# A hybrid attention layer on one core: another form and place for the layer norm's last steps, and another written order of the steps before it

## The chip, the cores and the metric

The kernel runs on one core of one Trainium2 chip. Its engines are named as the profile names them: PE multiplies matrices, and PEld is its loading of weights; DVE (VectorE) and ACT (ScalarE) work element by element; POOL (GpSimd) does so too and issues some of the transfers; SP issues the others. SBUF is the memory that all of them use, PSUM the memory into which PE writes. The metric is the device time of one execution in microseconds (us); lower is better.

## The reference

One layer for 512 tokens of width 1024: a projection, three mixers (an attention of three branches for 6 heads, a stick-breaking attention for 4, a gated recurrence for 6), gates, an output projection with the residual, and a layer norm.

```python
def layer_norm(v, g, b):
    v32 = v.astype(jnp.float32)
    mu = jnp.mean(v32, axis=-1, keepdims=True)
    var = jnp.mean(jnp.square(v32 - mu), axis=-1, keepdims=True)
    return ((v32 - mu) * lax.rsqrt(var + LN_EPS) * g + b).astype(v.dtype)

def reference(x, w_in, cmp_pos, w_ck1, w_ck2, w_cv1, w_cv2, hg_lb, hg_norm_w,
              w_out, ln_g, ln_b, rel_bias):
...
        h = x @ w_in[l]
...
        o_nsa = nsa_mixer(nsa_q, nsa_kc, nsa_vc, nsa_ks, nsa_vs, nsa_kw, nsa_vw, nsa_g,
                          cmp_pos[l], w_ck1[l], w_ck2[l], w_cv1[l], w_cv2[l], rel_bias)
        o_sb = stick_breaking_mixer(sb_q, sb_k, sb_v)
        o_hg = hgrn2_mixer(hg_q, hg_f, hg_i, lb_all[l])
...
        mixed = jnp.concatenate([o_nsa * jax.nn.silu(nsa_z),
                                 o_sb * jax.nn.silu(sb_z),
                                 o_hg.astype(x.dtype) * jax.nn.silu(hg_z)], axis=-1)
        x = layer_norm(ALPHA * x + (mixed @ w_out[l]).astype(x.dtype), ln_g[l], ln_b[l])
    return x
```

## The kernel before, in words

Every large product is computed in three products of rounded parts: a matrix is split into a high part `hi` (ACT rounds it) and a low part `lo` (what is left), and hi·hi, hi·lo and lo·hi are summed in PSUM. `SPLITS` says for each group of weights, first half and second half, who makes `lo`: 0 is POOL, 1 is DVE, and 3 (also the default) is ACT, which writes -hi, and a transfer issued by POOL that adds the raw weights to it.

The work is cut into steps, written as Python generators: `x`, `hf1`, `hq`, `hi`, `sq` and the like are blocks of the projection, `p0` to `p2` the pairs of heads of the recurrence, `s0` to `s3` and `v0` to `v3` the stick-breaking heads, `ck`, `cv`, `c0`, `c1`, `n0` to `n11` and `w0` to `w11` the attention, `o0` and `o1` the parts of the output projection that need only the last five of eight row blocks, and `end` the rest of it with the layer norm. The string `ORDER` lists in which order the steps advance; a name with L ahead starts a load. A scheduler then makes each engine's own order from it: what is written earlier has priority, and what stands under `high_priority` goes ahead of it where it is ready. At run time each engine takes its instructions strictly in that order and waits where one isn't ready.

`ENGINES` says for small operations whether DVE ('v'), POOL ('p') or ACT ('a') does them: `hq` and `hv0` to `hv2` copy blocks of the projection out of PSUM, `kb0` to `kb2` are the sums `nk` of the recurrence, `qs1` a product in it, `mz2` a gate product ahead of `end`.

`end` multiplies four tiles of 128 tokens (`i` is 0 to 3) by two halves of the width (`half`), adds each to `y[i, half]` in SBUF, and takes the layer norm of a tile when both halves are there. `norm_stats` sums on DVE (`bn`, then `mv`) and gets `rs`, the reciprocal root, from ACT. `norm_apply` scales and shifts y on ACT, multiplies by `ln_g` and adds `ln_b`, on DVE or POOL, and sends y out; for the last tile DVE does it all, in four instructions of two steps each. The gains `ln_g` and shifts `ln_b` lie in SBUF as four tiles named `ln`. The last half of the last tile comes from PE in two parts of 256 columns.

Of the kernel before, what the change touches and what calls it, by code (L numbers as in the profile page):

```python
# [14 lines left out]
ALU = mybir.AluOpType  # L15
# [8 lines left out]
NT = S // P  # L24
# [28 lines left out]
)  # L53

ORDER = (
# [7 lines left out]
)  # L63

BUFS = dict(at=3, g2=33, kkp=4, ma=2, mb=4, nb=2, p0=1, p5=4, psa=3, psc=1, raw=3, sa=8, sb=6, ta=8, tb=10, ti=1,
    w=16)

SPLITS = dict(ck=(0, 1), cv=(0, 1), hf1=(1, 1), hi=(3, 0), hi_sv=(0, 3), hq=(0, 0), hz=(1, 3), kw_sz=(1, 1),
    o0=(1, 3), o2=(0, 0), o3=(1, 1), sk=(3, 1), sq=(1, 3), sv_vs=(3, 1), vc_ks=(1, 3))

FROM_DRAM = ('sq', 'sk', 'q', 'q_kc', 'o0', 'o2', 'o4', 'o6')

ENGINES = dict(cl='p', e20='v', e21='p', hq='a', hs='v', hv0='v', hv1='a', hv2='a', k1='a', kb0='v', kb1='v',
    kb2='v', kd0='v', kt='v', mz0='v', mz1='v', mz2='p', mz3='v', mz4='v', nw0='v', nw1='v', nw2='v', q1='p', qs0='p',
    qs1='p', qs2='p', tmpta='a', tmptb='v', ts='p', z0='v', z1='a', z2='a', z3='v')
POOL_TILES = (1, 3)
LN_VECTOR = ((0, 1), (2, 0), (2, 1))
WARM = 8
LEVELS = (64, 32, 16, 8, 4, 2, 1)
PLAIN = 32  # L80
# [46 lines left out]
class Net:  # L127
# [777 lines left out]
    def norm_stats(self, i):  # L905
        nc = self.nc
        n = S // 2 if i == NT - 1 else S
        st = self.small((P, DM // n, 6), s="bn")
        for e in range(DM // n):
            c = e * n % S  # L910
            nc.vector.bn_stats(out=st[:, e, :], in_=self.y[i, e * n // S][:, c:c + n])
        mv = self.small((P, 2), s="mv")
        nc.vector.bn_aggr(out=mv, in_=st)
        rs = self.small((P, 1), s="rs")
        nc.scalar.activation(rs, mv[:, 1:2], AF.Ln, bias=self.eps_ln)
        nc.scalar.activation(rs, rs, AF.Exp, scale=-0.5)
        nm = self.small((P, 1), s="nm")
        if i == NT - 1:
            nc.vector.tensor_scalar(out=nm, in0=mv[:, 0:1], scalar1=-1.0, scalar2=None, op0=ALU.mult)
        else:  # L920
            nc.vector.tensor_scalar(out=nm, in0=mv[:, 0:1], scalar1=rs, scalar2=-1.0, op0=ALU.mult, op1=ALU.mult)
        return rs, nm

    def norm_apply(self, i, rs, nm):
        nc = self.nc
        y = [self.y[i, e] for e in range(2)]
        for e in range(2):
            if i == NT - 1:
                nc.vector.scalar_tensor_tensor(out=y[e], in0=y[e], scalar=nm, in1=self.lng[e], op0=ALU.add, op1=ALU.mult)
                nc.vector.scalar_tensor_tensor(out=y[e], in0=y[e], scalar=rs, in1=self.lnb[e], op0=ALU.mult, op1=ALU.add)  # L930
            else:
                nc.scalar.activation(y[e], y[e], AF.Identity, scale=rs, bias=nm)
                eng = nc.vector if (i, e) in LN_VECTOR else nc.gpsimd
                eng.tensor_tensor(out=y[e], in0=y[e], in1=self.lng[e], op=ALU.mult)
                nc.gpsimd.tensor_tensor(out=y[e], in0=y[e], in1=self.lnb[e], op=ALU.add)
            nc.sync.dma_start(out=self.out[0, i * P:(i + 1) * P, e * S:(e + 1) * S], in_=y[e])


# [230 lines left out]
    def do_end(self):  # L1169
        nc, a = self.nc, self.a  # L1170
        self.lng, self.lnb = [], []
        for l, n in ((self.lng, "ln_g"), (self.lnb, "ln_b")):
            for e in range(2):
                t = self.g2(s="ln")
                nc.sync.dma_start(out=t, in_=a[n][0:1, e * S:(e + 1) * S].broadcast_to([P, S]))
                l.append(t)
        ws = [self.out_weights(0, 2, half) for half in range(2)]
        mid = [self.out_weights(2, 1, half) for half in range(2)]
        for kt in range(3):
            self.do_m(kt)  # L1180
        st = {}
        for i in range(NT):
            for half in range(2):
                self.out_part(i, half, {0: ws[half]}, {2: mid[half]}, 2 if (i, half) == (NT - 1, 1) else 1)
            st[i] = self.norm_stats(i)
            if i:
                self.norm_apply(i - 1, *st[i - 1])
        self.norm_apply(NT - 1, *st[NT - 1])


def build(tc, a, out):
# [31 lines left out]
```

## Time and profile before

| what | value |
|---|---|
| time, median of 3 runs | 369.04 us (368.83 to 369.29) |
| the profiled execution's own time | 368.77 us |
| its span, first to last instruction | 366.9 us |
| outside the span | 1.9 us |
| PE busy | 343.1 us (94%) |
| DVE busy | 276.8 us (75%) |
| ACT busy | 248.1 us (68%) |
| POOL busy | 103.8 us (28%) |
| TensorE clock granted, mean | 0.99 |

The span is the time on the core; the runs' time adds some 2 us around it. Busy shares are means over stages with different limits, and PE's busy time counts products that overlap, so it is no measure of PE at its best rate.

### The profile page before, as it was taken

Reading aid. Unit: us, or ns where it says so; the run is one execution under the profiler, and the core shown is the slowest. Engines: PE = TensorE matmul, PEld = TensorE weight load, DVE = VectorE, ACT = ScalarE, POOL = GpSimd, SP = SyncE. Lnnn points to the kernel's source line nnn. Section 1 sums busy time; section 2 is a strip of 40 time slices with the busy share of each in tenths; the row PEclk is TensorE's granted clock in tenths of the full one; section 3 lists DMA queues with packets and bytes.
Section 4 is the critical chain, followed back from the end, with each engine's and each line's share of the span. In section 5 each row is a group of like instructions: output and inputs, shape, how many; then the busy total and the mean of one; then the engine's idle time right before and its main releaser. Section 6 shows DMA issues by size and latency. Waiting matters only on the chain.

```text
span 366.9 us, 5871 instructions
## 1 busy us (share of the span) xinstructions
PE 343.1 (94%) x2002; PEld 290.4 (79%) x2002; DVE 276.8 (75%) x628; ACT 248.1 (68%) x559; POOL 103.8 (28%) x145
## 2 busy tenths in 40 slices
PE   7999999999999998998999998999999899999980
PEld 5787899887888876876788997977877777888870
DVE  2769666689699888898876666788999657732796
ACT  3696963728559998785396777688889988731240
POOL 4065560001201111020471332242131604031092
PEclk9999999999999999999999999999999999999995
DMA  7767365250415472051348619500040698961023
GB/s 244 264 230 198 103 187 155 80 138 2 114 59 126 106 181 49 0 134 41 103 137 210 184 33 223 174 29 2 29 107 10 128 250 223 289 179 22 1 88 143
DMA packets 16910, 45.64 MB, mean 124 GB/s; under 512 B 2786, under 2 KB 3298, under 8 KB 16880
## 3 DMA queue, kind: packets, MB, share of 16 engines
q1 hardware_dynamic: 13568, 33.65, 27.5%
q0 software_dynamic: 3312, 11.61, 17.8%
q8 instruction: 16, 0.26, 0.3%
q14 instruction: 14, 0.11, 0.1%
HBM read 37.27 MB, written 2.14 MB: 107 GB/s over the span
## 4 chain that ended last, share of the span: by engine, by line
PE 56%; DVE 14%; ACT 11%; issue 10%; DMA 5%; POOL 3%; SPq 0%; DVEq 0%; POOLq 0%; ACTq 0%
PE pi L329 16%; PE pi L345 11%; PE pi L902 10%; PE pc L402 3%; PE ma L811 3%; DMA lo<-raw 3%; PE ma L377 2%; PE mb L395 2%; PE pi L316 2%; DVE sr L702 2%; DVE qz L806 2%; DMA xt<-xt 2%; ACT hi L273 2%; DVE att L820 1%; ACT pt L650 1%
## 5 line engine op out<-in xcount | busy, mean ns | idle before, releaser
L329 PE MATMUL pi<-xh,hi 128*128 128x512 f32 x160 | 47.8, 406 | 1.8 <-DVE vs L186 1.3
L329 PE MATMUL pi<-xh,lo 128*128 128x512 f32 x160 | 46.5, 396 | 1.4 <-DMA lo<-raw 1.4
L329 PE MATMUL pi<-xl,hi 128*128 128x512 f32 x160 | 46.6, 397 | 0.0
L902 PE MATMUL pi<-hi,mx 128*128 128x512 f32 (+1 forms) x134 | 40.9, 383 | 0.0
L329 PEld LDWEIGHTS pi<-xh,lo 128*128 128x128 f32 x160 | 29.3, 188 | 7.4 <-DMA lo<-raw 2.2
L329 PEld LDWEIGHTS pi<-xh,hi 128*128 128x128 f32 x160 | 28.5, 189 | 7.4 <-DVE vs L186 1.7
L329 PEld LDWEIGHTS pi<-xl,hi 128*128 128x128 f32 x160 | 29.3, 188 | 5.4
L186 DVE TENSOR_TENSOR pl<-mb,ph 128x384 fp32r<-128x384 f32 (+1 forms) x48 | 28.1, 595 | 6.8 <-ACT ph L185 6.3
L345 PE MATMUL pi<-lo,xh 128*128 128x256 f32 (+1 forms) x160 | 27.6, 286 | 1.5 <-DMA lo<-raw 1.3
L345 PE MATMUL pi<-hi,xh 128*128 128x256 f32 (+1 forms) x160 | 28.1, 290 | 0.6 <-DVE vs L186 0.6
L902 PEld LDWEIGHTS pi<-hi,mx 128*128 128x128 f32 x134 | 24.8, 188 | 4.5
L273 ACT CAST hi<-raw 128x1024 fp32r<-128x1024 f32 (+2 forms) x23 | 23.3, 1013 | 7.0 <-PE pi L902 2.8
L680 POOL TENSOR_SCALAR pt<-pt,sm,gates 128x256 f32<-128x256 f32 (+1 forms) x24 | 17.6, 740 | 33.5 <-DVE sm L677 29.3
L345 PE MATMUL pi<-hi,xl 128*128 128x256 f32 (+1 forms) x160 | 26.7, 284 | 0.0
L650 ACT ACTIVATE pt<-pt,mn 128x256 f32<-128x256 f32 (+3 forms) x42 | 24.5, 586 | 2.4 <-DVE mn L648 2.2
L902 PE MATMUL pi<-lo,mx 128*128 128x512 f32 (+1 forms) x67 | 25.8, 385 | 0.0
L185 ACT CAST ph<-mb 128x384 fp32r<-128x384 f32 (+1 forms) x48 | 24.0, 508 | 1.5 <-PE mb L395 1.3
L345 PEld LDWEIGHTS pi<-hi,xh 128*128 128x128 f32 x160 | 23.0, 190 | 1.6 <-DVE vs L186 0.8
L345 PEld LDWEIGHTS pi<-lo,xh 128*128 128x128 f32 x160 | 22.7, 191 | 1.9 <-DMA lo<-raw 1.5
L811 PEld LDWEIGHTS ma<-qz,kz 128*128 128x128 f32 x168 | 20.8, 191 | 3.7 <-ACT kz L795 1.1
L648 DVE CUSTOM_DVE_ANT_0 pt<-ma,nb 128x256 f32<-128x256 f32 (+3 forms) x42 | 21.2, 511 | 3.4 <-PE ma L377 3.3
L811 PE MATMUL ma<-qz,kz 128*128 128x128 f32 x168 | 22.7, 279 | 1.0 <-ACT kz L795 0.4
(269 smaller groups left out, 845.9 us busy)
## 6 DMA issues: line engine op xcount, KB each, us to landing
raw<-w_in SPq DMA_DIRECT2D x28, 512.0 KB, 3.6
lo<-raw POOLq DMA_DIRECT2D x9, 512.0 KB, 5.1
lo<-w_in POOLq DMA_DIRECT2D x6, 512.0 KB, 5.4
raw<-w_out SPq DMA_DIRECT2D x6, 512.0 KB, 5.1
lo<-w_out POOLq DMA_DIRECT2D x5, 512.0 KB, 5.4
y<-x SPq DMA_DIRECT2D x8, 256.0 KB, 4.2
out<-y SPq DMA_DIRECT2D x8, 256.0 KB, 2.0
xt<-xt SPq DMA_DIRECT2D x3, 512.0 KB, 7.2
```

Of the source, the lines that this page charges most:

```text
L185: nc.scalar.copy(hi, src)
L186: nc.vector.tensor_tensor(out=lo, in0=src, in1=hi.bitcast(F32), op=ALU.subtract)
L273: nc.scalar.copy(hi, raw)
L316: self.nc.tensor.matmul(ps, w[:, c0:c0 + P], self.xpart(x, kt), start=(n == 0 and j == 0), stop=(n == len(parts) - 1 and j == len(js) - 1))
L329: self.nc.tensor.matmul(ps, w[:, b * P:(b + 1) * P], self.xpart(x, kt), start=(n == 0 and j == 0), stop=(n == len(grp) - 1 and j == len(js ...
L345: self.nc.tensor.matmul(ps[:, :w_], self.xpart(x, kt)[:, i * P:(i + 1) * P], w[:, :w_], start=(j == 0), stop=(j == len(js) - 1))
L402: nc.tensor.matmul(acc[:, j * P:], vt[j], t[:, b:b + w], start=(first and j == 0 and t is h), stop=(last and j == 3 and t is l))
L648: nc.vector.tensor_tensor_reduce(out=dst, in0=src, in1=self.nb[h][:, n - 1::-1], scale=1.0, scalar=3e38, op0=ALU.add, op1=ALU.min, accum_o ...
L650: nc.scalar.activation(dst, dst, AF.Exp, bias=mn, scale=-1.0, accum_out=sm)
L680: (nc.gpsimd if i in POOL_TILES else nc.vector).tensor_scalar(out=pts[i], in0=pts[i], scalar1=sm[:, i:i + 1], scalar2=self.gates[:, i, c:c ...
L811: nc.tensor.matmul(ps[:, c * P:(c + 1) * P], kk[:, c * P:(c + 1) * P], qz[:, c, :, :].rearrange("p h t -> p (h t)"), start=True, stop=True)
L902: nc.tensor.matmul(ps, m, w[:, cs], start=(j == 0), stop=(j == len(jobs) - 1))
```

## The change

It does four things. The gains and shifts of the layer norm are also copied to PSUM (four new ACT instructions, tiles of the pool `mb`), and DVE's instructions of the layer norm read them there, while POOL's read the tiles in SBUF as before; which engine multiplies and adds for each tile and half stays as it was (`LN_FORM` writes out what `LN_VECTOR` and the test for the last tile said). In `end`, the statistics and the four last instructions of tile 3 are written under high priority. The tables `SPLITS` and `ENGINES` change: DVE takes over the `hq` copies and the `hv1` copies from ACT, and `qs1` and `mz2` from POOL; POOL takes `kb0` and `kb2` from DVE; the low parts of `hi`, `hi_sv`, `sq`, `o2` and of the second half of `o6` get other makers. And `ORDER` is another string. In all, DVE gets 11 instructions more (641 for 630), ACT 4 fewer, POOL 4 fewer, PE the same 1860 in the program.

```diff
 ORDER = (
-    "x Lhf1 Lhq 4*hf1 3*hq Lhi_sv 3*hi_sv Lhi hi_sv p1 hi Lsq hq hi p1 p0 hi 2*p1 const p1 hi 3*p1 sq p1 p0 sq 2*p0 "
+    "x Lhf1 Lhq 4*hf1 3*hq 3*hi_sv Lhi hi_sv Lhi_sv p1 hi hq hi Lsq 2*p1 p0 hi 2*p1 const p1 hi 3*p1 p0 2*sq Lsk sq "
...
-    "n10 n11 2*w9 n11 w9 m3 n10 n11 nz n10 w10 n11 2*w10 w11 nz w11 nz Lnz w11 o0 nz 3*o0 4*o1 end "
+    "2*n10 2*w9 2*n11 n10 m3 n11 nz w9 w10 n11 2*w10 w11 Lnz 2*nz w11 nz o0 w11 2*o0 o1 o0 3*o1 end "
...
-SPLITS = dict(ck=(0, 1), cv=(0, 1), hf1=(1, 1), hi=(3, 0), hi_sv=(0, 3), hq=(0, 0), hz=(1, 3), kw_sz=(1, 1),
-    o0=(1, 3), o2=(0, 0), o3=(1, 1), sk=(3, 1), sq=(1, 3), sv_vs=(3, 1), vc_ks=(1, 3))
+SPLITS = dict(ck=(0, 1), cv=(0, 1), hf1=(1, 1), hi=(0, 3), hi_sv=(1, 3), hq=(0, 0), hz=(1, 3), kw_sz=(1, 1),
+    o0=(1, 3), o2=(1, 1), o3=(1, 1), o4=(3, 3), o6=(3, 1), sk=(3, 1), sq=(3, 1), sv_vs=(3, 1), vc_ks=(1, 3))
...
-ENGINES = dict(cl='p', e20='v', e21='p', hq='a', hs='v', hv0='v', hv1='a', hv2='a', k1='a', kb0='v', kb1='v',
-    kb2='v', kd0='v', kt='v', mz0='v', mz1='v', mz2='p', mz3='v', mz4='v', nw0='v', nw1='v', nw2='v', q1='p', qs0='p',
-    qs1='p', qs2='p', tmpta='a', tmptb='v', ts='p', z0='v', z1='a', z2='a', z3='v')
+ENGINES = dict(cl='p', e20='v', e21='p', hq='v', hs='v', hv0='v', hv1='v', hv2='a', k1='a', kb0='p', kb1='v',
+    kb2='p', kd0='v', kh='a', kt='v', mz0='v', mz1='v', mz2='v', mz3='v', mz4='v', nw0='v', nw1='v', nw2='v', q1='p',
+    qs0='p', qs1='v', qs2='p', tmpta='a', tmptb='v', ts='p', z0='v', z1='a', z2='a', z3='v')
...
-LN_VECTOR = ((0, 1), (2, 0), (2, 1))
+LN_FORM = (("pp", "vp"), ("pp", "pp"), ("vp", "vp"), ("s", "s"))
...
-            if i == NT - 1:
-                nc.vector.scalar_tensor_tensor(out=y[e], in0=y[e], scalar=nm, in1=self.lng[e], op0=ALU.add, op1=ALU.mult)
-                nc.vector.scalar_tensor_tensor(out=y[e], in0=y[e], scalar=rs, in1=self.lnb[e], op0=ALU.mult, op1=ALU.add)
+            m = LN_FORM[i][e]
+            if m == "s":
+                nc.vector.scalar_tensor_tensor(out=y[e], in0=y[e], scalar=nm, in1=self.lngp[e], op0=ALU.add, op1=ALU.mult)
+                nc.vector.scalar_tensor_tensor(out=y[e], in0=y[e], scalar=rs, in1=self.lnbp[e], op0=ALU.mult, op1=ALU.add)
             else:
                 nc.scalar.activation(y[e], y[e], AF.Identity, scale=rs, bias=nm)
-                eng = nc.vector if (i, e) in LN_VECTOR else nc.gpsimd
-                eng.tensor_tensor(out=y[e], in0=y[e], in1=self.lng[e], op=ALU.mult)
-                nc.gpsimd.tensor_tensor(out=y[e], in0=y[e], in1=self.lnb[e], op=ALU.add)
+                for f, g, gp, op in zip(m, (self.lng[e], self.lnb[e]), (self.lngp[e], self.lnbp[e]), (ALU.mult, ALU.add)):
+                    if f == "v":
+                        nc.vector.tensor_tensor(out=y[e], in0=y[e], in1=gp, op=op)
+                    else:
+                        nc.gpsimd.tensor_tensor(out=y[e], in0=y[e], in1=g, op=op)
...
+        self.lngp, self.lnbp = [], []
+        for l, lp in ((self.lng, self.lngp), (self.lnb, self.lnbp)):
+            for t in l:
+                lp.append(self.ps("mb"))
+                nc.scalar.copy(lp[-1], t)
...
-            st[i] = self.norm_stats(i)
-            if i:
+            if i == NT - 1:
+                with self.tc.high_priority():
+                    st[i] = self.norm_stats(i)
                 self.norm_apply(i - 1, *st[i - 1])
-        self.norm_apply(NT - 1, *st[NT - 1])
+                with self.tc.high_priority():
+                    self.norm_apply(i, *st[i])
+            else:
+                st[i] = self.norm_stats(i)
+                if i:
+                    self.norm_apply(i - 1, *st[i - 1])
```

Three places show what this makes of the engines' orders. The first is DVE at the very end. Tile 3 is `y_3777` and `y_3873` before, `y_3815` and `y_3872` after; the two halves of tile 2 are `y_3758` with `y_3854` or `y_3853`; `pi` is PE's result, `ln` and `mb` are the gains and shifts. Before:

```order
L903 SCALAR_TENSOR_TENSOR y_3873<-y_3873,pi_4060 128x256
L911 BN_STATS bn_4082<-y_3777 128x6
L911 BN_STATS bn_4082<-y_3873 128x6
L903 SCALAR_TENSOR_TENSOR y_3873<-y_3873,pi_4071 128x256
L934 TENSOR_TENSOR y_3758<-y_3758,ln_3892 128x512
L911 BN_STATS bn_4082<-y_3873 128x6
L934 TENSOR_TENSOR y_3854<-y_3854,ln_3894 128x512
L913 BN_AGGR mv_4087<-bn_4082 128x2
L919 TENSOR_SCALAR nm_4092<-mv_4087 128x1
L929 SCALAR_TENSOR_TENSOR y_3777<-y_3777,nm_4092,ln_3892 128x512
L929 SCALAR_TENSOR_TENSOR y_3873<-y_3873,nm_4092,ln_3894 128x512
L930 SCALAR_TENSOR_TENSOR y_3777<-y_3777,rs_4089,ln_3896 128x512
```

The same place of the change:

```order
L912 BN_STATS bn_4089<-y_3815 128x6 x2
L904 SCALAR_TENSOR_TENSOR y_3872<-y_3872,pi_4067 128x256
L937 TENSOR_TENSOR y_3758<-y_3758,mb_3899 128x512
L912 BN_STATS bn_4089<-y_3872 128x6
L904 SCALAR_TENSOR_TENSOR y_3872<-y_3872,pi_4078 128x256
L937 TENSOR_TENSOR y_3853<-y_3853,mb_3901 128x512
L912 BN_STATS bn_4089<-y_3872 128x6
L914 BN_AGGR mv_4094<-bn_4089 128x2
L920 TENSOR_SCALAR nm_4099<-mv_4094 128x1
L931 SCALAR_TENSOR_TENSOR y_3815<-y_3815,nm_4099,mb_3899 128x512
L931 SCALAR_TENSOR_TENSOR y_3872<-y_3872,nm_4099,mb_3901 128x512
L932 SCALAR_TENSOR_TENSOR y_3815<-y_3815,rs_4096,mb_3903 128x512
```

Both products of tile 2 still stand ahead of tile 3's `mv`; each has moved up, and the first now stands ahead of the last addition of `pi`. What DVE reads as `ln` in SBUF it now reads as `mb` in PSUM.

The second place is ACT where the attention ends and `o0` runs: `ph` are casts that the last `w` steps wait for, `zz` a gate. Before:

```order
L185 CAST ph_3605<-mb_3601 128x384
L185 CAST ph_3618<-mb_3613 128x512
L426 ACTIVATE zz_3732<-zz_3732 128x512
L185 CAST ph_3648<-mb_3644 128x384
L185 CAST ph_3670<-mb_3666 128x384
L142 COPY tmp_3678<-pc_3572 64x512
L283 CAST hi_3901<-raw_3900 128x1024
```

The same place of the change:

```order
L186 CAST ph_3605<-mb_3601 128x384
L186 CAST ph_3618<-mb_3613 128x512
L1186 COPY mb_3899<-ln_3891 128x512
L186 CAST ph_3660<-mb_3656 128x384
L1186 COPY mb_3901<-ln_3893 128x512
L186 CAST ph_3728<-mb_3724 128x384
L1186 COPY mb_3903<-ln_3895 128x512
L1186 COPY mb_3905<-ln_3897 128x512
L143 COPY tmp_3736<-pc_3572 64x512
```

The four new copies stand between the last casts, in tiles of the pool `mb` that the casts' inputs use too.

The third place is DVE early in the program, where the recurrence starts: `e`, `kz` and `qz` are its small factors, `z` its first column, `hq` the query that `z` and `qz` need. Before:

```order
L751 SCALAR_TENSOR_TENSOR b_350<-rst_170,bb_341 128x512
L799 TENSOR_TENSOR e_882<-b_281 128x128x2
L753 TENSOR_TENSOR nk_352<-ab_335,b_350 128x512
L784 TENSOR_TENSOR z_395<-key_255,hq_380 64x4 x2
L793 TENSOR_TENSOR kz_401<-nk_283,b_281 128x512
L793 TENSOR_TENSOR kz_402<-nk_283,b_281 128x4x65
L793 TENSOR_TENSOR kz_403<-nk_263,b_261 128x512
L784 TENSOR_TENSOR z_396<-key_275,hq_450 64x4 x2
```

The same place of the change:

```order
L752 SCALAR_TENSOR_TENSOR b_350<-rst_170,bb_341 128x512
L145 COPY hq_380<-pi_355 128x512
L800 TENSOR_TENSOR e_882<-b_281 128x128x2
L785 TENSOR_TENSOR z_395<-key_255,hq_380 64x4 x2
L794 TENSOR_TENSOR kz_401<-nk_283,b_281 128x512
L794 TENSOR_TENSOR kz_402<-nk_283,b_281 128x4x65
L794 TENSOR_TENSOR kz_403<-nk_283,b_281 128x8x33
L145 COPY hq_450<-pi_425 128x512
L785 TENSOR_TENSOR z_396<-key_275,hq_450 64x4 x2
```

Two `hq` copies have come in, one `nk` has gone to POOL, and a `kz` of another level and pair stands in its place.

## Rows read from the trace of the kernel before

**Rows 1.** The page: busy time, share of the span and instructions of each engine.

```profile
PE 343.1 (94%) x2002; PEld 290.4 (79%) x2002; DVE 276.8 (75%) x628; ACT 248.1 (68%) x559; POOL 103.8 (28%) x145
```

**Rows 2.** Stretches: busy us (instructions) per engine, clock, DMA share, GB/s.

```profile
20.00:80.00 60.00, 60.00 (x402) 53.38 (x401) 42.96 (x80) 38.47 (x82) 24.07 (x32) 1.00 0.58 159
80.00:190.00 110.00, 103.44 (x602) 86.15 (x601) 97.68 (x203) 81.40 (x183) 20.37 (x27) 1.00 0.34 85
...
300.00:320.00 20.00, 19.91 (x106) 15.99 (x107) 14.87 (x32) 16.40 (x36) 5.10 (x7) 1.00 0.90 246
320.00:356.50 36.50, 36.43 (x170) 30.34 (x168) 20.48 (x37) 12.11 (x21) 12.97 (x11) 1.00 0.29 79
356.50:367.00 10.50, 0.00 (x0) 0.00 (x0) 7.32 (x10) 0.68 (x3) 3.60 (x3) 0.63 0.34 126
```

**Rows 3.** Chain that ended last, from 319.76 us: start, us, what.

```profile
319.76 34.54 PE pi L902 x152
```

**Rows 4.** Timeline of DVE, the end: start, us, engine line op tiles.

```profile
354.32 0.69 DVE L903 SCALAR_TENSOR_TENSOR y<-y,pi 128x512 f32<-128x512 f32 x1 [0.38 <-PE pi L902]
...
355.05 0.42 DVE L911 BATCH_NORM_STATS2 bn<-y 128x6 f32<-128x256 f32 x1
355.39 0.42 DVE L903 SCALAR_TENSOR_TENSOR y<-y,pi 128x256 f32<-128x256 f32 x1
355.73 0.75 DVE L911 BATCH_NORM_STATS2 bn<-y 128x6 f32<-128x256 f32 x2
356.47 0.42 DVE L903 SCALAR_TENSOR_TENSOR y<-y,pi 128x256 f32<-128x256 f32 x1
356.81 1.32 DVE L934 TENSOR_TENSOR y<-y,ln 128x512 f32<-128x512 f32 x1
358.05 0.41 DVE L911 BATCH_NORM_STATS2 bn<-y 128x6 f32<-128x256 f32 x1
358.39 1.63 DVE L934 TENSOR_TENSOR y<-y,ln 128x512 f32<-128x512 f32 x1
359.94 0.25 DVE L913 BATCH_NORM_AGGREGATE mv<-bn 128x2 f32<-128x24 f32 x1
...
360.41 2.16 DVE L929 SCALAR_TENSOR_TENSOR y<-y,nm,ln 128x512 f32<-128x512 f32 x2
362.49 1.40 DVE L930 SCALAR_TENSOR_TENSOR y<-y,rs,ln 128x512 f32<-128x512 f32 x2
```

**Rows 5.** Timeline of POOL over the same stretch.

```profile
353.70 1.29 POOL L935 TENSOR_TENSOR y<-y,ln 128x512 f32<-128x512 f32 x1
...
356.32 1.26 POOL L935 TENSOR_TENSOR y<-y,ln 128x512 f32<-128x512 f32 x1
358.21 1.26 POOL L935 TENSOR_TENSOR y<-y,ln 128x512 f32<-128x512 f32 x1 [0.63 <-DVE y L934]
360.10 1.26 POOL L935 TENSOR_TENSOR y<-y,ln 128x512 f32<-128x512 f32 x1 [0.63 <-DVE y L934]
```

**Rows 6.** Timeline of ACT over the same stretch.

```profile
355.17 1.52 ACT L932 ACTIVATE y<-y,nm,rs 128x512 f32<-128x512 f32 x2 [0.67 <-DVE nm L921]
```

**Rows 7.** ACT groups, 18 to 80 us: count, busy us, mean ns, idle before.

```profile
L142 ACT COPY hv<-pi 128x128 f32<-128x128 f32 x8 | 2.1, 261 | 6.1 <-DVE hv L144 3.9 <-PE pi L345 2.2
...
L142 ACT COPY hq<-pi 128x512 f32<-128x512 f32 x3 | 1.7, 582 | 0.0
```

**Rows 8.** DVE groups of the same stretch.

```profile
L285 DVE TENSOR_TENSOR lo<-raw,hi 128x1024 fp32r<-128x1024 f32 x4 | 4.9, 1221 | 2.1 <-ACT hi L283 1.3 <-PE pi L316 0.7
...
L753 DVE TENSOR_TENSOR nk<-ab,b 128x512 f32<-128x512 f32 x3 | 2.1, 686 | 0.1
```

**Rows 9.** Waits of PE, 100 to 320 us: total us, times, longest.

```profile
PE pi L329 <- DMA lo<-raw: 1.4, 2, 0.9
...
PE mb L395 <- ACT sz L704: 1.3, 2, 1.1
PE pi L329 <- DVE vs L186: 1.3, 1, 1.3
```

More of the change, by code (lines that the diff above doesn't have):

```diff
@@ L917, in norm_stats @@
         nm = self.small((P, 1), s="nm")
-        if i == NT - 1:
+        if LN_FORM[i] == ("s", "s"):
             nc.vector.tensor_scalar(out=nm, in0=mv[:, 0:1], scalar1=-1.0, scalar2=None, op0=ALU.mult)
@@ L927, in norm_apply @@
         for e in range(2):
-            if i == NT - 1:
-                nc.vector.scalar_tensor_tensor(out=y[e], in0=y[e], scalar=nm, in1=self.lng[e], op0=ALU.add, op1=ALU.mult)
-                nc.vector.scalar_tensor_tensor(out=y[e], in0=y[e], scalar=rs, in1=self.lnb[e], op0=ALU.mult, op1=ALU.add)
+            m = LN_FORM[i][e]
+            if m == "s":
+                nc.vector.scalar_tensor_tensor(out=y[e], in0=y[e], scalar=nm, in1=self.lngp[e], op0=ALU.add, op1=ALU.mult)
+                nc.vector.scalar_tensor_tensor(out=y[e], in0=y[e], scalar=rs, in1=self.lnbp[e], op0=ALU.mult, op1=ALU.add)
             else:
                 nc.scalar.activation(y[e], y[e], AF.Identity, scale=rs, bias=nm)
-                eng = nc.vector if (i, e) in LN_VECTOR else nc.gpsimd
-                eng.tensor_tensor(out=y[e], in0=y[e], in1=self.lng[e], op=ALU.mult)
-                nc.gpsimd.tensor_tensor(out=y[e], in0=y[e], in1=self.lnb[e], op=ALU.add)
+                for f, g, gp, op in zip(m, (self.lng[e], self.lnb[e]), (self.lngp[e], self.lnbp[e]), (ALU.mult, ALU.add)):
[3 more added lines that the diff above has]
+                        nc.gpsimd.tensor_tensor(out=y[e], in0=y[e], in1=g, op=op)
             nc.sync.dma_start(out=self.out[0, i * P:(i + 1) * P, e * S:(e + 1) * S], in_=y[e])
```

10 rows, old and new, of the table ORDER are left out of this document.

## The prediction

> **What bounds the kernel now.** I read the page first: PE is busy 343.1 us [rows 1] of a span of 366.9, so PE's stream is the frame, and what can change is the time in which it stands and the time after it has ended. The table of stretches shows where that is. From 20 to 80 us PE is busy 60.00 of 60; from 80 to 190 it misses 6.6 us (110 less 103.44), and there DVE is busy 97.68 of 110, so PE waits for a DVE and an ACT that are nearly full; from 320 to 356.5 it misses 0.1; in the last 10.5 us it does nothing and DVE works 7.32 [rows 2]. The chain that ended last confirms the end: 152 products of the output projection without a break from 319.76 us [rows 3], one each 0.227 us (34.54 / 152), and then DVE alone. The list of what PE waits for between 100 and 320 us has many small entries and none large: the greatest are 1.3 to 1.4 us in one or two pieces, on a transfer of a low part, on ACT's `sz`, on a DVE split [rows 9]. So no single wait carries the middle; the end has a single owner, DVE.
>
> The end, read from DVE's timeline [rows 4]: the last addition of `pi` starts at 356.47 and takes 0.42. Then come a product of tile 2 (1.32 us), a `bn`, the second product (1.63), `mv`, and the four last instructions, 2.16 for the first two and 1.40 for the others, which end at 363.89. The span ends 3.0 us later, with the transfer of the last y. The same form of two reads, done in 0.70 each at the end, takes 1.32, 1.63 and 1.08 where POOL is adding: POOL's rows run from 356.32 to 357.58, 358.21 to 359.47 and 360.10 to 361.36 [rows 5]. Each time DVE's instruction ends 0.55 us after POOL's (356.81 + 1.32 = 358.13; 358.39 + 1.63 = 360.02), and the pair from 360.41 finishes 1.2 us after. The addition of `pi` at 354.32, which reads one input from PSUM, took 0.69 although POOL was adding from 353.70 to 354.99 [rows 4, 5].
>
> **The change part by part.**
>
> *The end.* Six instructions on the chain get one input from PSUM: two products and the four last ones. No row shows this product with PSUM. Its nearest rows are the addition of `pi` at 0.69 and the product itself beside POOL, 1.63 at most [rows 4]; I take 0.69, since two inputs with one in PSUM is its form, and POOL at work is its situation. I lay the new order on the old times, with the start-to-start steps of the rows: 0.34 for a `bn` or an addition of 256 columns (355.05 to 355.39, 356.47 to 356.81), 0.47 from `mv` to the first of the four (359.94 to 360.41). Two `bn` at 355.05 and 355.39, the addition at 355.73, the first product at 356.07 (ACT has its input ready at 355.17 + 0.76 = 355.93 [rows 6]), a `bn` at 356.76, the last addition at 357.10 (0.63 later than before, since the product stands ahead of it), the second product at 357.44, the last `bn` at 358.13, `mv` at 358.47, the four from 358.94 at 0.70 each: end at 361.74. That is 2.15 us before 363.89. POOL's additions for tile 2 follow the products and end by 360.1 (357.58 + 2 x 1.26 = 360.10), ahead of the first output of tile 3, so they don't become the end. High priority itself gives nothing by this reckoning: the order shows both products still ahead of tile 3's `mv`, and 1.4 us of them in its chain. Bounds: with the products at 1.63 and the four at 1.08 each, 361.74 + 2 x 0.94 + 4 x 0.38 = 365.1, a loss of 1.3; in the other direction the DVE work that the chain cannot shed leaves at most some 0.3 more.
>
> [...]
>
> *The copies into PSUM.* Four ACT instructions of 128x512, not shown in the trace; the nearest row, a copy of that shape, is 0.58 [rows 7], so 2.3 in all. They stand between the last casts of `w11`, between 300 and 320 us, where ACT is busy 16.40 of 20 [rows 2]. I cost them at nothing: 3.6 us of ACT are idle there, and PE has `o0` to do, missing 0.1 us in that stretch. Without the cover a cast behind a copy is late, then the low part on DVE, then PE's product; at most the whole 2.3.
>
> *Who does what.* From 20 to 80 us DVE takes three `hq` copies (0.69 each, by the addition of `pi`, since a plain copy of that shape isn't shown), four `hv` copies (0.26 each, from ACT's row), one low part more (1.22) and `qs1` (taken as 0.58), and loses two `nk` (0.69 each) [rows 4, 7, 8]: 2.07 + 1.04 + 1.22 + 0.58 - 1.37 = 3.5 us. ACT sheds 3 x 0.58 + 4 x 0.26 = 2.8. I take nothing for it: DVE has 17 us idle there and PE isn't waiting [rows 2]. Without that slack, `hq` comes late, then `z` and `qz` queued behind it on DVE, then PE's products for `p1`: up to 3.5. A gain there would need a PE wait to remove, and there is none. Near the end, DVE takes the two low parts of `o2` from POOL and `mz2`, three instructions of 0.69, 2.1 in all; DVE is idle 16 of 36.5 us from 320 on, and covers it; else up to 2.1.
>
> *The loads.* SP now issues all of `y` and `ln` (12 times 256 KB, 3.1 MB) ahead of the last four weight loads (1.5 MB), two of which stood before `y`. The last 72 products start 72 x 0.227 = 16.3 us before PE's end, at 340. At the 246 GB/s of 300 to 320 us [rows 2], 4.7 MB take 19 us from the time when `y` may load, which falls in that stretch; even from 315 they are in by 334. Cost nothing; else as much as the weights are late.
>
> *The order of the steps.* PE's order changes between about 50 and 190 us and again around 300 to 320; in between it is nearly the same. The work of DVE in the full stretch of 80 to 190 is about the same, since what moved lies before 80 or after 300 (one low part of `sq` changes sides, in the first half to a transfer, in the second back). So the new order can only turn the 6.6 us of PE's idle time over: bounds -6.6 and, as a wait of the same size again, +6.6. I take 0.
>
> **Sum.** 366.9 - 2.15 = 364.75 of span, 366.6 with the 1.9 around it for the profiled execution (368.77 before); the median of the runs was 0.27 above that, so 369.04 - 2.2 = 366.8.
>
> **The rivals.** What can be told from no change is about 0.2%, 0.74 us.
>
> A, *the order removes waits*: it takes half of PE's idle time from 80 to 190 us as well, 3.3 us: 363.5. For it, PE waits there in many pieces that a written order can move; against it, DVE at 89% leaves little room.
>
> B, *the PSUM operand is not cheaper beside POOL*: the products stay at 1.3 to 1.6 and the pair at 1.08, and moving the products up gains little: some -0.3, 368.7. Against it stands the 0.69 at 354.32.
>
> C, on the other side, *DVE early*: the 3.5 us added to DVE before 80 us don't find its gaps, and the recurrence enters the full stretch later by that. PE then pays it once: 366.8 + 3.5 = 370.3. It is slower than before from 2.9 us (2.15 + 0.74) of the 3.5 on. For it, `hq` now waits its turn on an in-order DVE, with `z` behind it; against it, the 17 idle us.
>
> D, *the copies into PSUM come through*: 2.3 us of ACT in front of the last casts, or their tiles of `mb` missing to them: 366.8 + 2.3 = 369.1, no change. For it, they stand between casts that PE needs; against it, `o0`.
>
> E, *the new order costs half of what the end gives*, in new waits of some 1.1 us between 80 and 190: 367.9.
>
> **How the numbers follow.** Forecast 0.45 (366.1 to 367.5), A 0.18, E 0.07, B 0.09, D 0.08, C 0.13. Faster is forecast, A and E: 0.70; the same, B and D: 0.17; slower, C: 0.13. The likeliest is 366.8. The range from 364.0 to 369.6 leaves out C and a part of A, some 0.2; above, the case of D fits in it with room for its 2.3 and a little more.
>
> **What would show it.** Right: DVE's four last instructions at about 0.70 each and the two products at about 0.69 beside POOL's additions; from the end of PE to the end of DVE 5.3 us instead of 7.5; PE's idle time from 80 to 190 us within 1 us of 6.6 and PE still unbroken from 320 on. For A, PE's end comes 2 us or more earlier. For B, products over 1.2 us. For C, PE idle between 50 and 110 us behind DVE's `hq` or `qz`. For D, PE idle behind `ph` from 305 to 320. Wrong altogether would be a PE that ends some us later or earlier for a wait that stands in none of these rows.

## The result, and the profile after

The changed kernel takes 363.78 us (median of 4 runs, 362.77 to 364.19) where the kernel before takes 368.96 (368.83 to 369.29): a ratio of 0.9854, 95% interval 0.9833 to 0.9876, 5.2 us less. Its profiled execution took 363.92, with a span of 362.1. The forecast was 366.8, with a range from 364.0 to 369.6, so the time lies 0.2 us below the range.

The page, the busy row that answers to [rows 1]:

```profile
PE 343.2 (95%) x2002; PEld 292.1 (81%) x2002; DVE 280.1 (77%) x639; ACT 246.9 (68%) x555; POOL 97.2 (27%) x141
```

The stretches, with the columns of [rows 2] (busy us of PE, PEld, DVE, ACT, POOL, then clock, DMA share, GB/s):

```profile
20.00:80.00 60.00, 60.00 (x402) 53.36 (x401) 46.24 (x87) 36.18 (x74) 24.21 (x32) 1.00 0.57 159
80.00:190.00 110.00, 105.12 (x622) 88.91 (x621) 98.69 (x206) 84.80 (x188) 20.70 (x27) 1.00 0.34 88
...
300.00:320.00 20.00, 20.00 (x108) 16.36 (x107) 15.36 (x32) 17.01 (x35) 3.78 (x5) 1.00 0.89 265
320.00:354.00 34.00, 33.99 (x159) 28.33 (x157) 21.00 (x38) 10.77 (x20) 8.93 (x8) 1.00 0.20 55
```

PE does the same work, and misses 4.9 us from 80 to 190 instead of 6.6; DVE and ACT get more done there (98.69 and 84.80 instead of 97.68 and 81.40). The chain that ended last has the same kind of piece as in [rows 3], 147 products of the output projection instead of 152, and it ends earlier:

```profile
318.41 33.45 PE pi L903 x147
```

DVE's end, which answers to [rows 4] (the code's lines stand one to three further down: the products are L937, the four last L931 and L932):

```profile
352.61 0.75 DVE L912 BATCH_NORM_STATS2 bn<-y 128x6 f32<-128x256 f32 x2
353.28 0.41 DVE L904 SCALAR_TENSOR_TENSOR y<-y,pi 128x256 f32<-128x256 f32 x1
353.60 0.68 DVE L937 TENSOR_TENSOR y<-y,mb 128x512 f32<-128x512 f32 x1
354.19 0.42 DVE L912 BATCH_NORM_STATS2 bn<-y 128x6 f32<-128x256 f32 x1
354.53 0.40 DVE L904 SCALAR_TENSOR_TENSOR y<-y,pi 128x256 f32<-128x256 f32 x1
354.85 0.68 DVE L937 TENSOR_TENSOR y<-y,mb 128x512 f32<-128x512 f32 x1
355.45 0.42 DVE L912 BATCH_NORM_STATS2 bn<-y 128x6 f32<-128x256 f32 x1
355.90 0.26 DVE L914 BATCH_NORM_AGGREGATE mv<-bn 128x2 f32<-128x24 f32 x1
...
356.39 1.41 DVE L931 SCALAR_TENSOR_TENSOR y<-y,nm,mb 128x512 f32<-128x512 f32 x2
357.71 1.40 DVE L932 SCALAR_TENSOR_TENSOR y<-y,rs,mb 128x512 f32<-128x512 f32 x2
```

POOL over the same stretch, as in [rows 5]:

```profile
349.64 7.72 POOL L939 TENSOR_TENSOR y<-y,ln 128x512 f32<-128x512 f32 x6 [0.19 <-ACT y L934]
```

POOL adds without a gap until 357.36. Beside it the two products take 0.68 each, and the first pair of the four last instructions takes 1.41, where before they took 1.32, 1.63 and 2.16: with one operand in PSUM each takes 0.68 to 0.71 beside POOL's additions. The second pair runs after POOL has ended and took 1.40 before as well. The three differences, 0.64, 0.95 and 0.75, add up to 2.34 us. Next, compare where PE stands. One product marks the end of the full stretch, the first of the attention `c0`; before and after it reads:

```profile
206.98 0.62 PE L617 MATMUL ma<-q,kc 128*96 128x512 f32 x2
```

```profile
203.94 0.62 PE L618 MATMUL ma<-q,kc 128*96 128x512 f32 x2
```

Such marks cut every execution into five parts, worked out from the starts and ends in its trace: the start (to PE's 61st product, which is the same work in all), from there to the mark, from the mark to PE's end, from there to DVE's end, and what follows (3.02 us in all). Before they are 17.36, 189.62, 149.45, 7.46, 3.02. Differences to these, with the timed ratio:

```
                          start  to c0  to PE's end  to DVE's end   median us  ratio (95%)
after                      +0.3   -3.4     +0.6        -2.3          363.78    0.9854 (0.9833-0.9876)
e1  end only               -0.0   +0.1     +0.0        -2.3          366.58    0.9914 (0.9880-0.9947)
e12 end, no priority       +0.3   +0.0     +0.0        -2.4          366.78    0.9932 (0.9918-0.9947)
e15 priority only          +0.2   +0.1     +0.0        -0.8          368.43    0.9978 (0.9970-0.9987)
e2  tables only            +0.4   -3.4     +0.8        +0.1          366.61    0.9914 (0.9887-0.9941)
e3  ORDER only             +0.4   -3.3     +0.3        +0.1          366.38    0.9913 (0.9887-0.9940)
e4  makers only            +0.3   -0.0     +0.3        +0.0          369.38    0.9995 (0.9979-1.0011)
e17 ORDER and end          +0.6   -3.3     +1.6        -2.3          365.37    0.9900 (0.9884-0.9915)
e5  steps 1-50             +0.4   -0.1     +4.0        +0.0          372.17    1.0084 (1.0064-1.0104)
e6  steps 51-74            +0.5   -2.3     +2.2        +0.0          370.29    1.0035 (1.0020-1.0050)
e7  steps 75-100           +2.2   +0.9     +4.4        +0.0          373.48    1.0141 (1.0115-1.0166)
e8  steps 101-248          +0.4   -0.0     +0.9        +0.1          369.51    1.0021 (1.0005-1.0037)
e10 steps 1-50, buffer     +0.1   +0.5     -0.0        +0.0          369.32    1.0009 (1.0000-1.0018)
e18 steps 51-100, end      +0.9   -1.0     +0.5        -2.3          366.29    0.9928 (0.9903-0.9954)
e11 steps 1-100            +0.7   -3.1     +0.4        +0.0          366.34    0.9923 (0.9910-0.9936)
e9  two steps swapped      -0.4   +1.9     +5.8        +0.0          375.46    1.0179 (1.0160-1.0198)
e13 e9, nz's lo on DVE     +0.3   +1.7     +5.2        +0.0          374.79    1.0145 (1.0125-1.0166)
e14 after, nz's lo on DVE  +2.4   -3.4     +6.2        -2.3          369.96    1.0029 (1.0010-1.0048)
e16 after, nz and hz       +0.0   -3.4     +8.1        -2.3          373.48    1.0106 (1.0076-1.0135)
```

The start column belongs to one execution and not to the kernel: it lies between -0.4 and +0.9, and at +2.2 and +2.4 in two whose kernels do nothing new there. So the other columns tell more than one execution's time. The executions of e6 and e16 that were profiled took 369.03 and 371.04, less than the medians, so their columns add up to less.

Between the 61st product and the mark PE has the same products to do. These are the two stretches, before and after, with the columns of [rows 2]:

```profile
17.36:206.98 189.62, 183.06 (x1111) 156.66 (x1109) 151.62 (x308) 134.71 (x294) 50.78 (x64) 1.00 0.45 118
```

```profile
17.70:203.94 186.24, 181.37 (x1110) 156.45 (x1109) 154.74 (x318) 131.89 (x287) 50.29 (x65) 1.00 0.45 120
```

Of the 3.4 us won there only 1.7 are idle time of PE (6.56 before, 4.87 after). The other 1.7 are busy time of the same work. The two products at the mark show why: together they take 0.62, which is 0.39 for one product and 0.23 from the start of one to the start of the next, so that some 0.16 us of a wait behind a product count as busy. The idle time breaks PE's stream 19 times before and 10 times after; nine times 0.16 is 1.4 us, an estimate of what the busy row hides.

### The profile page after: what moved, and what is told of

Its sections match the earlier page's. It is cut to its first block, busy times and chain, and to the rows that moved or that the text cites. A ratio compares the mean times of both kernels' runs of the same rounds, so it can differ in the third digit from the quotient of the medians.

```text
span 362.1 us, 5875 instructions
## 1 busy us (share of the span) xinstructions
PE 343.2 (95%) x2002; PEld 292.1 (81%) x2002; DVE 280.1 (77%) x639; ACT 246.9 (68%) x555; POOL 97.2 (27%) x141
## 4 chain that ended last, share of the span: by engine, by line
PE 69%; DVE 13%; ACT 7%; issue 4%; DMA 4%; POOL 1%; DVEq 0%; SPq 0%; ACTq 0%; POOLq 0%
PE pi L330 22%; PE pi L903 12%; PE pi L346 11%; PE pc L403 4%; PE ma L812 4%; PE pi L317 4%; PE mb L396 3%; PE ma L378 3%; DMA lo<-raw 3%; DVE ct L509 2%; DVE sr L703 2%; PE ma L860 1%; DVE att L821 1%; DVE sz L704 1%; PE pc L1137 1%
## 5 line engine op out<-in xcount | busy, mean ns | idle before, releaser
L330 PE MATMUL pi<-xl,hi 128*128 128x512 f32 x160 | 45.5, 394 | 0.0
L275 ACT ACTIVATE lo<-hi 128x1024 fp32r<-128x1024 f32 (+2 forms) x22 | 22.4, 1020 | 4.3 <-PE pi L903 4.0
L279 POOL DMA_DIRECT2D lo<-raw x12 | 10.6, 880 | 50.5 <-ACT lo L275 29.0
L274 ACT CAST hi<-raw 128x1024 fp32r<-128x1024 f32 (+2 forms) x22 | 22.2, 1011 | 2.5 <-PE pi L330 1.5
```

The costliest lines, as they stand in the source:

```text
L274: nc.scalar.copy(hi, raw)
L275: nc.scalar.activation(lo, hi.bitcast(F32), AF.Copy, scale=-1.0)
L330: self.nc.tensor.matmul(ps, w[:, b * P:(b + 1) * P], self.xpart(x, kt), start=(n == 0 and j == 0), stop=(n == len(grp) - 1 and j == len(js ...
```

## The experiments

All are compared with the kernel before on the same chip. "Steps" are the 248 of `ORDER`, counted from its start; pieces were cut where both orders have done the same steps.

**The parts by themselves.** e1 takes the new end into the kernel before, e2 the three tables, e3 `ORDER` alone, e4 `SPLITS` and `ENGINES` alone:

```diff
 e1: LN_FORM, the copies to PSUM, high priority      as after; ORDER, SPLITS, ENGINES as before
 e2: ORDER, SPLITS, ENGINES                          as after; the end as before
 e3: ORDER                                           as after; all else as before
 e4: SPLITS, ENGINES                                 as after; all else as before
```

e1: 

> The kernel before with the new end alone: the four copies into PSUM, the operands of DVE's layer norm read from there, the high priority; ORDER, SPLITS and ENGINES as before. Theory 1 (the two gains add up: the end gives what was forecast, the rest of the 5.2 us comes from the middle): 366.7 us, 2.2 to 2.4 below before, PE's last product at 356.4 as before, and 5.1 us from there to DVE's end. Theory 2 (the new order is needed for the end to gain): within 0.7 us of before. Theory 3 (the copies into PSUM get in front of the last casts): PE's end 0.5 to 2.3 us later, and 367.2 to 369.

e2: 

> The kernel before with the three tables of the change, ORDER, SPLITS and ENGINES, and its own end. Theory 1 (the gains add up): 366.5 us, PE's last product at 354.0 as in the kernel after, then 7.5 us to DVE's end as before. Theory 2 (without the copies into PSUM on ACT ahead of the last casts PE loses less between 285 and 320 us): PE's end at 353.0 to 353.5 and 365.6 to 366.0. Theory 3 (the tables give nothing alone): 369.

e3: 

> The kernel before with the new ORDER alone; SPLITS, ENGINES and the end as before. Theory A (the written order takes away the waits of PE between 80 and 190 us): 366.0 to 366.6, with PE some 3 us ahead of before by 190 us. Theory B (who copies and who makes low parts takes them away): 369 within 0.7. Theory C (order and makers were fitted to one another, and either alone is worse): 370 or more.

e4: 

> The kernel before with the new SPLITS and ENGINES alone; ORDER and the end as before. Theory A (the order): 369 within 0.7. Theory B (the makers): 366.0 to 366.6, with PE some 3 us ahead of before by 190 us. Theory C (fitted to one another): 370 or more.

Theory 1 held in e1 and e2, theory A in e3 and e4: the end gives 2.3 us behind PE's end and nothing elsewhere; `ORDER` gives 3.3 ahead of the mark; the makers alone give nothing. 0.9914 x 0.9913 is 0.983, 0.3% below the 0.9854 of the whole change, which is what their intervals leave open (e17 below puts the two together). In e2 PE lost no less after the mark than in the kernel after (+0.8 and +0.6), so its theory 2 fell.

**What in the end does it.** e12 keeps the PSUM operands and drops the priority; e15 keeps the priority and the order and reads SBUF:

```diff
-            if i == NT - 1:
-                with self.tc.high_priority():
-                    st[i] = self.norm_stats(i)
...
+            st[i] = self.norm_stats(i)
```

```diff
-                nc.vector.scalar_tensor_tensor(out=y[e], in0=y[e], scalar=nm, in1=self.lngp[e], op0=ALU.add, op1=ALU.mult)
+                nc.vector.scalar_tensor_tensor(out=y[e], in0=y[e], scalar=nm, in1=self.lng[e], op0=ALU.add, op1=ALU.mult)
```

e12: 

> The kernel before with the four copies into PSUM and the operands read there, in the old place and without the high priority. Theory 1 (the PSUM operand gives the whole gain of the end, the priority nothing): 366.6, like the run with the whole new end, with the products at 0.68 us and the four last at 0.70 each. Theory 2 (the priority is what gains): 369.

e15: 

> The kernel before with the high priority and the new place of tile 3's last steps, and the operands in SBUF as before; no copies into PSUM. Theory 1 (the PSUM operand gives the whole gain of the end): 369 within 0.7. Theory 2 (either alone gives it, since a higher place takes tile 3's work out of POOL's way): 367.5 or less.

e12 has the whole gain. In e15 0.8 of the 2.3 us are there; its 368.43 lies at the low edge of theory 1's range (369 within 0.7), but its interval leaves out no change, so the priority gives a little by itself. DVE's rows there show why it is no more:

```profile
356.31 0.76 DVE L937 TENSOR_TENSOR y<-y,ln 128x512 f32<-128x512 f32 x1
...
357.65 1.09 DVE L937 TENSOR_TENSOR y<-y,ln 128x512 f32<-128x512 f32 x1
...
359.61 2.48 DVE L931 SCALAR_TENSOR_TENSOR y<-y,nm,ln 128x512 f32<-128x512 f32 x2
```

The products moved up and take less time (0.76 and 1.09 instead of 1.32 and 1.63 [rows 4]), but the pair behind them takes more, 2.48 instead of 2.16. With PSUM operands the products take 0.68 and 0.67 in the old place too, and the pair 1.41 (e12), so the place no longer matters.

**Where in the order.** Four pieces, each alone in the kernel before:

```diff
 e5: steps 1 to 50 of ORDER as after, 51 to 248 as before
 e6: steps 51 to 74 as after       e7: steps 75 to 100 as after       e8: steps 101 to 248 as after
```

e5: 

> The kernel before with the first 50 of the 248 steps of ORDER as in the change, the others as before. Theory 1 (the 3 us of the order are many small waits, won along the whole stretch): 367.9 to 368.4, with PE about 1 us ahead by 105 us. Theory 2 (one place carries them): 366.4, or 369.3 if it isn't here. Theory 3 (the stretches only fit as a whole): 370 or more.

e6: 

> The same for steps 51 to 74, with the attention's scores and the four stick-breaking heads. Theory 1: 368.3 to 368.8, some 0.7 us won. Theory 2: 366.4, or 369.3 if the place isn't here. Theory 3: 370 or more.

e7: 

> The same for steps 75 to 100. Here lies the single longest stall of PE before, 1.44 us at 138 us, and the one of 1.22 us at 170. Theory 1: 367.9 to 368.4. Theory 2: 366.4, or 369.3 if the place isn't here. Theory 3: 370 or more.

e8: 

> The same for steps 101 to 248, the whole rest. In the run with the whole new order PE lost 0.3 to 0.7 us of its lead after 190 us, most of it between 290 and 325. Theory 1: 369.3 to 370.0, no gain or a small loss. Theory 2: 366.4, or 369.3 if the place isn't here. Theory 3: 370 or more.

Each alone loses, 0.6 to 4.6 us in the medians: theory 3 in e5, e6 and e7, theory 1 in e8. The losses of e5, e6 and e7 lie behind the mark for the most part (e7 loses 0.9 ahead of it, e6 wins 2.3), and have one place in common: the wait of PE that ends at 294.80 before and takes 0.48 us there takes 2.53, 2.42 and 2.47. The SP queue shows what changed. Before, a load of w_out starts at 270.56:

```profile
270.56 25.05 SPq L269 DMA_DIRECT2D raw<-w_out  x4
```

In e5, e6 and e7 it starts at 288 us or later, with the next one right behind it, because the scheduler gave it another of the three `raw` buffers, one that a low part's transfer still reads. e9 makes that happen by itself, and e10 undoes it in e5. The waits of the SP queue from 255 to 292 us show the two buffers; before, the load behind the one at 270.56 waits for ACT, and in e9 the first one waits for a transfer:

```profile
SPq L269 <- ACT hi L273: 18.8, 1, 18.8
```

```profile
SPq L269 <- DMA lo<-raw: 19.1, 1, 19.1
```

The two edits:

```diff
 e9, ORDER of before:        - ... vc_ks p2 ck kw_sz ...     + ... vc_ks ck p2 kw_sz ...
 e10, e5's ORDER further on: - ... 2*v1 s0 v1 Lq_kc ...      + ... v1 s0 2*v1 Lq_kc ...
```

e9: 

> The kernel before with two neighbouring steps of ORDER swapped, p2 and ck (at about 185 us), and nothing else. The three runs that lost most with a piece of the order all had one thing in common: SP's load of w_out that starts at 270.56 us before started only at 288 to 290, in a buffer of raw that a transfer of a low part still used, and PE then waited 2.6 to 2.7 us at about 294 us for that transfer instead of 0.6. This swap gives the load the same late buffer, and changes PE's order only from 185 to 225 us. Theory 1 (the buffer that a load gets decides): 370.4 to 372.5, with that load at 285 us or later and a stall of 2 us or more at about 294. Theory 2 (the losses come from the early pieces themselves): 369 within 0.7.

e10: 

> The run with steps 1 to 50 of the new ORDER (372.2) once more, with two neighbouring steps further on swapped, v1 and s0, which gives the load of w_out the early buffer again, as in the kernel before. Theory 1 (the buffer): 368.3 to 369.5, with the load at about 270 us and no stall over 1 us at about 294. Theory 2 (the piece itself loses): 371.5 to 372.8.

Theory 1 held in e10, which loses nothing behind the mark. In e9 its signs are there (the late load, and a stall of 2.6 us), but not its time: e9 loses 6.5 us for two steps, 3 more than theory 1 allowed. Its SP queue, PE's waits from 185 to 330 us, and the chain that ended last:

```profile
293.31 8.05 SPq L269 DMA_DIRECT2D raw<-w_out  x4
```

```profile
PE pi L329 <- DMA lo<-raw: 3.5, 2, 2.6
PE pi L345 <- DMA lo<-raw: 1.8, 1, 1.8
PE mb L580 <- DMA w<-w_ck: 0.8, 1, 0.8
```

```profile
292.92 7.62 DMA lo<-raw
```

The low part that PE waits for took 7.62 us, beside the first two of those four loads (the two others start at 300.56 and later). In the chain of before, beside one load, it is

```profile
289.25 5.50 DMA lo<-raw
```

Ahead of that, e9 lost 1.9 us up to the mark and some 2 more by 240 us, which it had not been built to cause. The last two of PE's rows are a part of it (the first of these was 1.3 before), and behind the wait of 1.8 the granted clock fell to 0.69 from 225 to 230 us, as the last section shows; the rest has no row here. So the late buffer stands for 3.6 of e9's 6.5 us.

**Whether the gains add.** e11 takes steps 1 to 100, e18 steps 51 to 100 with the new end; in both the load has its early buffer:

e11: 

> The kernel before with steps 1 to 100 of the new ORDER, and the old steps 101 to 248. The load of w_out has the early buffer in it. Theory 1 (the pieces' early gains add up, and the buffer made their losses): 365.4 to 366.5, with PE 3 to 4 us ahead by 190 us. Theory 2 (the early gains need the new late steps): 369 or more.

e18: 

> The kernel before with steps 51 to 100 of the new ORDER and the new end; the first 50 steps, the steps from 101 on and the makers as before. The load of w_out has the early buffer. By the piece runs, steps 51 to 74 had won 2.7 us by 190 us, steps 75 to 100 0.5, steps 1 to 50 1.2. Theory 1 (the pieces' early gains add): 363.4 to 364.2, some 5.2 below before. Theory 2 (steps 1 to 50 are what makes the rest work): 366 or more.

e11 has the whole gain, so the 148 later steps give nothing that can be measured. e18 has 1.0 of the 3.3 to the mark, and its time is that of the end alone: theory 2, against what I had read from the pieces. Steps 1 to 50 alone give nothing (e10, +0.5 to the mark), 51 to 100 1.0, both together 3.1. Steps 51 to 74 alone had 2.3 at the mark (e6) and 75 to 100 alone lost 0.9 (e7); e6 with the early buffer was not run.

**The transfers behind it.** If the stall in e9 is that transfer, making the low part on DVE should take it away, and the like stalls of the kernel after with it (1.5 us for `nz`, 1.6 for `hz`):

```diff
 e13 (e9) and e14 (after):  + nz=(3, 1)       e16 (after):  + nz=(3, 1)   - hz=(1, 3)   + hz=(1, 1)
```

e13: 

> The run with the two swapped steps (375.5), and the low part of the second half of the weights nz made by DVE instead of by ACT and a transfer. Theory 1 (the 2.8 us stall at about 298 us, and the half clock after it, come from that transfer, which took 7.6 us beside three loads of w_out instead of 5.5): 371.5 to 372.5, without that stall and with the clock at 1.00 all along. Theory 2 (PE waits there for something else that is late): 375 within 0.8. The 3.6 us that the swap costs between 180 and 240 us stay by either.

e14: 

> The kernel after, with the low part of the second half of the weights nz made by DVE instead of by ACT and a transfer. PE's longest stall late in the kernel after is 1.69 us at 290.7 us, for that transfer. Theory 1 (a wait on it alone): 362.0 to 362.8. Theory 2 (DVE's own work there is as late): 363.8 within 0.7.

e16: 

> The kernel after, with DVE making the low parts of the second halves of both nz and hz. PE's stall at 218.9 us (1.76) is for the transfer of hz. A load of w_out gets another buffer by it, one that waits for a transfer. Theory 1 (both stalls go, and the buffer doesn't matter once PE waits for no transfer there): 360.0 to 361.5. Theory 2 (the late load takes back what the stalls gave): 362.5 to 365.

Theory 1 failed in all three. The time of e13 lies in its theory 2's range, those of e14 and e16 are far above both ranges. The stalls that they aimed at are gone or down to 0.3, and the next low part is late instead. PE's waits in e13 and in e14:

```profile
PE pi L902 <- DMA lo<-w_out: 2.7, 1, 2.7
```

```profile
PE pi L903 <- DMA lo<-w_out: 5.3, 1, 5.3
```

In e14 the transfer of `o0`'s low part starts at 303.53 instead of 296.92, because ACT comes to that part's -hi later. ACT's row in the kernel after, then in e14, and two stretches of e14:

```profile
295.56 1.06 ACT L275 ACTIVATE lo<-hi 128x1024 fp32r<-128x1024 f32 x1
```

```profile
302.19 1.05 ACT L275 ACTIVATE lo<-hi 128x1024 fp32r<-128x1024 f32 x1
```

```profile
295.00:300.00 5.00, 5.00 (x31) 4.10 (x30) 4.36 (x16) 3.72 (x12) 0.00 (x0) 1.00 0.38 74
300.00:305.00 5.00, 5.00 (x28) 4.21 (x27) 2.60 (x8) 5.00 (x9) 2.40 (x3) 1.00 0.40 115
```

The DMA engines are busy only 0.38 and 0.40 of that time, so the transfer isn't late for want of their rate: taking one low part from ACT made the scheduler put the next one later in ACT's order. Why it did so is not shown, and so these edits don't tell what the stall itself costs. No version here beats the kernel after.

**The makers beside the rest.**

```diff
 e17: ORDER, LN_FORM, the copies to PSUM, high priority as after; SPLITS, ENGINES as before
```

e17: 

> The kernel after with the SPLITS and ENGINES of before: the new ORDER and the new end alone. Theory 1 (the makers give nothing, the two others add): 363.3 to 363.9, a ratio of 0.983 to 0.986 to before. Theory 2 (the makers are needed beside the two others): 364.5 or more.

Theory 2: without the makers 1.6 us are lost, 1.0 of it between the mark and PE's end. ACT's rows in e17 show where:

```profile
316.20 0.59 ACT L1186 COPY mb<-ln 128x512 f32<-128x512 f32 x1 [1.58 <-DMA ln<-ln_g]
316.73 0.47 ACT L186 CAST ph<-mb 128x384 fp32r<-128x384 f32 x1
318.74 0.59 ACT L1186 COPY mb<-ln 128x512 f32<-128x512 f32 x1 [1.54 <-DMA ln<-ln_g]
319.27 0.47 ACT L186 CAST ph<-mb 128x384 fp32r<-128x384 f32 x1
```

Two copies into PSUM wait 1.58 and 1.54 us for the gains to arrive, a cast is queued behind each, and PE waits for one of them:

```profile
PE pc L403 <- ACT ph L186: 1.1, 1, 1.1
```

In the kernel after the same copy starts when ACT comes to it, and PE waits for no cast:

```profile
314.08 0.59 ACT L1186 COPY mb<-ln 128x512 f32<-128x512 f32 x1
```

In e1, with the old order and the old makers, the copies wait too, and it costs nothing, since there they stand behind the last casts:

```profile
321.75 0.59 ACT L1186 COPY mb<-ln 128x512 f32<-128x512 f32 x1 [1.36 <-DMA ln<-ln_g]
```

So the loss needs three things at once: the copies, the new order that puts them between the casts, and the old makers. The wait of 1.1 us is the loss behind the mark; the other 0.6 us have no row.

## Why the prediction was wrong, point by point

**The end: right.** From PE's end to DVE's end it takes 5.1 us, with 5.3 forecast and 7.46 before. The products take 0.68 beside POOL's additions, the four last 0.70 each. The row on which it rested, an addition of `pi` beside POOL at 0.69 [rows 4, 5], spoke for this form. With one operand in PSUM these instructions of 512 columns take 0.68 to 0.70, and the last two of before, with both in SBUF, 0.70 each [rows 4]. Rival B is out. That the priority gives nothing holds beside the PSUM operands (e12); by itself it gives 0.8 (e15).

**The order of the steps: wrong, and this is the step that failed.** I bounded it by 6.6 us either way and took 0, because the work of DVE in the full stretch is about the same. It gives 3.3 us up to the mark and 2.95 in time (e3, 366.38 for 369.33). Rival A put just that at 3.3, with PE's end 2 us or more earlier (it is 2.4), and I gave it 0.18. That its number fits so well is partly luck: it was to be half of PE's idle time, and the idle time fell by 1.7, a quarter (4.9 from 80 to 190 us, where I had asked for 6.6 within 1); the other 1.7 came out of PE's busy time. So 6.6 was no bound either, since the idle row shows only a part of what waiting costs. ACT, which I called nearly full, was busy 81.40 of 110. The error is the inference from equal work to equal waiting: the waits on DVE's `vs` (1.3 of [rows 9], and another 0.6 of the same kind) are no longer in the list of after, where the greatest is another:

```profile
PE ma L812 <- ACT kz L796: 1.7, 1, 1.7
PE pi L346 <- DMA lo<-raw: 1.6, 1, 1.6
PE pi L330 <- DMA lo<-raw: 1.5, 1, 1.5
PE mb L396 <- DVE sr L702: 0.8, 1, 0.8
```

The gain that lasts needs both halves of the early order. Which inversion of steps does it, and why one half gives its lead back, is open.

**Who does what: right in the sum, for one reason too few.** DVE has 3.3 us more from 20 to 80 us (46.24 for 42.96 [rows 2]; 3.5 forecast), ACT 2.3 less; `qs1` takes 1.30 on DVE and not 0.58. All of it is hidden, e4 shows no change, and rival C is out. What I didn't see is that beside the copies into PSUM and the new order the makers are worth up to 1.6 us; which entry of the two tables does it was not tried.

**The copies into PSUM: right for this kernel, with the wrong price for the rival.** PE misses nothing from 300 to 320. D's mechanism is real (e17, with the old makers), but the price isn't 0.58 a copy: it is the wait for the copies' own load, 3.1 us of ACT, with the casts behind. I had listed the loads of y and ln as moved ahead of weights, at no cost, and not asked who waits for ln first.

**The loads, and the steps after 190: right that they add little.** PE loses 0.6 from the mark to its end, and is unbroken from 320 on. But these are the terms with the steepest loss beside them: a swap of two steps costs 6.5, of which the late load is 3.6.

## What to carry to other kernels

Where an order of steps feeds pools of few buffers, don't price it by the work that moves: read which buffer each load gets and what it waits for, since one load that moves by 20 us cost about as much here as the whole order gave (2.9 us between e5 and e10, for 2.95), and pieces of an order can each lose while the whole gains. Time an order and a change at the end apart, and cut the executions at marks of the same work: parts that add up told in one table what total times mixed. Don't take PE's idle time for all that waiting costs. And before one low part goes to another engine, read where that puts the next one in the order of the engine that prepares it.

## What the runs showed of the hardware

After PE's stall of 2.6 us, e9's granted clock read 0.70 over 5 us. The stretches of e9 (clock third from the end):

```profile
295.00:300.00 5.00, 2.96 (x14) 2.13 (x12) 1.28 (x3) 2.50 (x6) 2.08 (x3) 1.00 0.97 249
300.00:305.00 5.00, 4.41 (x18) 3.84 (x19) 1.85 (x4) 1.96 (x4) 0.00 (x0) 0.70 1.03 293
```

Products of 512 columns follow one another by 0.43 us in the second stretch and by 0.23 before the stall, as four of them show on either side:

```profile
296.26 1.07 PE L329 MATMUL pi<-xl,hi 128*128 128x512 f32 x4
...
302.80 1.91 PE L329 MATMUL pi<-xh,lo 128*128 128x512 f32 x4
```

If seven products lost 0.2 us each, that is some 1.4 us, an estimate from these two rows, by which the stall cost half as much again as it lasted. The same happened earlier in e9, behind the stall of 1.81 us that ends at 225.73:

```profile
225.00:230.00 5.00, 4.27 (x24) 4.27 (x25) 3.90 (x14) 3.26 (x13) 0.93 (x2) 0.69 1.03 229
```

The clock fell where the longest stalls of e5, e7, e14 and e16 (2.5 to 5.3 us) end as well: to 0.70 from 297.50 to 300 us in e5, to 0.68 from 310 to 315 in e14, and to 0.91 as a mean from 300 to 320 in e7 and in e16. It isn't the rule of every stall, and its length alone doesn't decide: behind e9's 1.81 us the clock fell, while e6 stood 2.42 us at the same place as e9's 2.6, and its clock stayed at

```profile
295.00:300.00 5.00, 4.85 (x29) 4.01 (x29) 2.44 (x7) 3.47 (x6) 0.46 (x1) 1.00 1.01 296
```

That is one execution of e6; the other eleven had mean clocks of 0.981 to 0.989, where this one had 0.993, and there is no trace of them.

And a transfer that adds 512 KB into a low part took 7.62 us beside two loads of w_out (e9) and 5.50 beside one (before); PE waited 2.63 us for the first and 0.48 for the second.
